# Weight blocks of 128x2048 instead of 128x1024 in a two-layer decoder, and what of it waits where

## The chip, the core and the metric

The kernel runs on one core of a Trainium2 chip. The metric is the device time of one execution in microseconds (us). Five engines work side by side and meet at semaphores: TensorE (PE in the profile, with PEld for its weight loads), VectorE (DVE), ScalarE (ACT), GpSimd (POOL) and SyncE (SP). DMA engines move data between DRAM and the on-chip memory; in this kernel SP issues the loads, POOL the loads that add to a tile, and ACT a few small ones.

## The reference

A decoder trunk of two layers on 256 tokens of width 2048. Layer 0 mixes tokens by gated linear attention, layer 1 by sliding-window attention; in both, four further heads attend to 256 memory tokens. A projection out, a residual and a squared-ReLU MLP (2048 to 8192 to 2048) follow. All in float32.

```python
for i in range(DEPTH):                                  # 2
    h = rmsnorm(x, attn_norm_g[i])
    mkv = mem_n @ w_mem_kv[i]                           # memory keys, values
    mk, mv = ...
    if i % 2 == 0:
        q, k, v, g_out, g_lr, xq = split(h @ w_in_gla)
        o_mix = rmsnorm(gla_mixer(q, k, v, g_lr, ...)) * silu(g_out)
    else:
        q, k, v, xq = split(h @ w_in_swa)
        o_mix = swa_sink_mixer(q, k, v, sinks)
    o_mem = memory_attention(xq, mk, mv)
    x = x + concatenate([o_mix, o_mem]) @ w_out[i]
    x = x + square(relu(rmsnorm(x) @ w_up[i])) @ w_down[i]
return rmsnorm(x, final_norm_g)
```

## The kernel before

**Every weight is used in two parts.** A weight block arrives in float32 (tile `wr`, by SP at L976), ACT copies it rounded to the format that TensorE reads (`wh`, the high half, L993), and DVE subtracts that copy from the block (`wl`, the low half, L994). Activations are stored split in the same way. A product is then three matmuls: high with high, high with low, low with high.

**Items.** The work is one list of items. An item is a block of 128 partitions by at most 1024 numbers, with what to do with it: load, perhaps a step before the split (`prep`), split, matmuls (`mm`), perhaps a step after the split (`then`). The main loop at the end of the kernel (L1013 to L1027) goes through the list with three leads: at item i it issues the load of item i+8 (LOAD_AHEAD), the `prep` of item i+5, the split of item i+3, then one step of each background task (softmax, gates, norms), then the matmuls of item i. There are 6 raw buffers (`wr`, WR) and 4 each of `wh` and `wl`. A scheduler then sets the order of the instructions on each engine, so this order is a plan and not the last word; the order shown below is that of the built program.

**The plans.** `fm_halves` (accumulators `p_acc`, `s_acc`; L198 and L199) makes two items for one block of 128 output columns: 8 pairs of a 512-wide and a 256-wide matmul each. `tm_halves` (`v_acc`, `o_acc`; L224 to L226) makes eight items for 512 output columns (388 for v), 12 matmuls each. `up` (L724 to L726) does the same for one of 16 up units of the MLP.

**Down projection.** It multiplies with sums of weight blocks: for each of seven groups e and each pair of column blocks, seven products take B11, T1, T2, B22, T3, T4 and B21 of the down weights (`FAST`, matmuls at L782 to L784). The T tiles are made by addition: `sum` is loaded with B11, then DVE adds B12 (`first_sum`, L828), then POOL adds B22 and later B21 by a DMA that accumulates (L825); `b12` is loaded with B12 and DVE adds the raw B22 block to it (`third_sum`, L831). Each accumulate must wait until the split of the sum before it is done. Group e is woven with the up units 2e+2 and 2e+3. The hidden units of an up unit pass through ACT and DVE (`q` at L755 to L758, `hid` at L762 and L763) before the down products read them. The last 1024 down rows go through `down_plain`.

**Start.** The first items of layer 0 are the x blocks and the v blocks, then memory blocks (`in_mem`, `in_mem_tok`, of which squares are taken, L141) placed among them and among the first gate, key and query blocks (`p0`, `p1`, ..., from `in_w_gla`). The memory keys and values of both layers are computed once in layer 0; those of layer 1 stay on the chip in `mk1` and `mv1`.

Of the kernel before, what the change touches and what calls it, by code (L numbers as in the profile page):

```python
# [16 lines left out]
P = 128  # L17
# [5 lines left out]
WR = 6  # L23
LOAD_AHEAD = 8
PREP_AHEAD = 5
SPLIT_AHEAD = 3
MEM_AT = (10, 15)
# [41 lines left out]
class Item:  # L69
# [5 lines left out]
    def __init__(self, src, width, split=None, mm=None, into=None, tile=None, prep=None, then=None):  # L75
        self.src, self.width, self.split, self.mm = src, width, split, mm
        self.into, self.tile, self.prep, self.then = into, tile, prep, then
# [3 lines left out]
def trunk_kernel(ctx: ExitStack, tc: tile.TileContext, a, out):  # L81
# [102 lines left out]
    def fm_halves(name, srcs, rhs, done, order=None):  # L184

        order = order or list(range(NK))
        st = {}

        def half(i):
            def mm(wh, wl):  # L190
                if i == 0:
                    st["acc"] = bank("main", name + "_acc")
                acc = st["acc"]
                r = rhs()
                for k in range(8):
                    kk = 8 * i + k
                    rk = r[order[kk]]
                    pe.matmul(acc, wh[:, k * P:(k + 1) * P], rk, start=kk == 0, stop=False, skip_group_check=True)  # L198
                    pe.matmul(acc[:, T:2 * T], wl[:, k * P:(k + 1) * P], rk[:, 0:T], start=False, stop=kk == NK - 1,  # L199
                              skip_group_check=True)  # L200
                if i == 1:
                    done(acc)
            return Item(srcs[i], 1024, mm=mm)

        return [half(0), half(1)]

    def tm_halves(name, srcs, n, lhs, done, order=None):
# [4 lines left out]
        def half(i):  # L212
            def mm(wh, wl):
                if i == 0:
                    st["acc"] = [bank("main", f"{name}_acc{t}") for t in range(2)]
                r = lhs()
                for t in range(2):
                    for k in range(2):
                        rk = r[order[2 * i + k]]
                        h, l = wh[:, k * n:(k + 1) * n], wl[:, k * n:(k + 1) * n]  # L220
                        first, last = 2 * i + k == 0, 2 * i + k == NK - 1
                        acc = st["acc"][t][:, 0:n]
                        hi, lo = rk[:, t * P:(t + 1) * P], rk[:, T + t * P:T + (t + 1) * P]
                        pe.matmul(acc, hi, h, start=first, stop=False)  # L224
                        pe.matmul(acc, hi, l, start=False, stop=False)  # L225
                        pe.matmul(acc, lo, h, start=False, stop=last)  # L226
                if i == 7:
                    done(st["acc"])
            return Item(srcs[i], 2 * n, mm=mm)

        return [half(i) for i in range(8)]

    def combine(acc, name):

        u = tp.tile([P, T], F32, tag="u", name=name + "_u")
        act.activation(u, acc[:, T:2 * T], AF.Copy)
        t = tp.tile([P, T], F32, tag="t", bufs=4, name=name + "_t")
# [18 lines left out]
    mkv = {1: [cp.tile([P, 4, T], F32, name="mk1"), cp.tile([P, 2, 512], F32, name="mv1")]}  # L256

    def act_item(src, first, n, key, gain, start=None):
# [9 lines left out]
        return Item(src, n * T, split=split)  # L268
# [21 lines left out]
    def x_task():  # L290

        for _ in range(4):
            yield
# [13 lines left out]
    def mem_halves(layer):  # L307
        hs = []

        def mv_done(accs):  # L310
            if layer == 0:
                S["mem_r"] = S["mem_st"].spread()
            for t in range(2):
                act.activation(mkv[layer][1][:, t, :], accs[t], AF.Copy, scale=S["mem_st"].tok[:, t:t + 1])

        hs += tm_halves(f"mv{layer}", [a["w_mv"][layer, i] for i in range(8)], 512, lambda: S["ms"], mv_done)
        for c in range(4):
            def mk_done(acc, c=c):
                t = combine(acc, f"mk{layer}{c}")
                dve.tensor_tensor(mkv[layer][0][:, c, :], t, S["mem_r"], ALU.mult)  # L320

            hs += fm_halves(f"mk{layer}{c}", [a["w_mk"][layer, c, i] for i in range(2)], lambda: S["ms"], mk_done)
# [40 lines left out]
    def gla_halves():  # L363
# [13 lines left out]
        vs = [tm_halves(f"v{g}", [a["w_v"][g, i] for i in range(8)], 388, lambda: S["xs"], v_done(g))  # L377
              for g in range(4)]
        for i in range(8):
            if i == 0:  # L380
                hs.append(act_item(a["x"][:, 0:2 * T], 0, 2, "xs", G_ATT))
            elif i == 1:
                hs.append(act_item(a["x"][:, 2 * T:4 * T], 2, 2, "xs", G_ATT))
            elif i % 2 == 0:
                hs.append(act_item(a["x"][:, 2 * i * T:(2 * i + 4) * T], 2 * i, 4, "xs", G_ATT))
            hs += [vs[0][i], vs[1][i]]
        rest = vs[2] + vs[3]
        extra = mem_items() + mem_stat_items()
        for i in range(16):
# [3 lines left out]
        def proj_done(job, idx):  # L393
            kind, h, j = job

            def f(acc):
# [15 lines left out]
                elif kind == "g":  # L412
                    sg = tp.tile([P, T], F32, tag="t", bufs=4, name=f"sg{idx}")
# [16 lines left out]
        for idx, job in enumerate(GLA_ORDER):  # L430
            if idx == 4:
                hs += mem_halves(0) + mem_halves(1)
            for h in fm_halves(f"p{idx}", [a["w_gla"][idx, i] for i in range(2)], lambda: S["xs"], proj_done(job, idx)):
                hs.append(h)
# [17 lines left out]
    def gla_task(h):  # L452
# [24 lines left out]
        ex = tp.tile([P, 2, P], F32, tag="t", bufs=4, name=f"ex{h}")  # L477
# [32 lines left out]
        for j in range(3):  # L510
# [6 lines left out]
            sq.append(tp.tile([P, T], F32, tag="sq", name=f"gsq{h}{j}", bufs=2))  # L517
# [8 lines left out]
        inv_sqrt(f"go{h}", b[:, 0:T], 1.0 / 384, r, *[tp.tile([P, T], F32, tag="t", bufs=4, name=f"go{h}_{z}") for z in "vw"])  # L526
# [6 lines left out]
    def start_swa():  # L533
# [14 lines left out]
        S["os"] = {}  # L548

# [76 lines left out]
    def swa_halves():  # L626
# [27 lines left out]
        jobs = [fm_halves(f"s{idx}", [a["w_swa"][idx, i] for i in range(2)], lambda: S["xs"], done(idx))  # L654
                for idx in range(len(SWA_COLS))]
        return late_start(jobs)


    def late_start(jobs):

        hs = [j[0] for j in jobs[0:3]] + [j[1] for j in jobs[0:3]]
        for j in jobs[3:]:
            hs += j
        return hs
# [22 lines left out]
    def out_halves(layer):  # L687
        hs = []
        for g in range(4):
            def done(accs, g=g):  # L690
# [3 lines left out]
            hs += tm_halves(f"o{layer}{g}", [a["w_out"][layer, g, i] for i in range(8)], 512, lambda: S["os"], done,  # L694
                            OUT_ROWS[layer])
        return hs

    def mlp_halves(layer):
# [9 lines left out]
        def up(n):  # L708

            st = {}  # L710

            def part(i):
                def mm(wh, wl):
                    if i == 0:
                        if n == 0:
                            open_phase()
                        st["acc"] = [bank("main" if n < 2 else "aux", f"u{layer}{n}_acc{t}") for t in range(2)]
                    for t in range(2):
                        for k in range(2):
                            rk = S["xs"][2 * i + k]  # L720
                            h, l = wh[:, k * 512:(k + 1) * 512], wl[:, k * 512:(k + 1) * 512]
                            hi, lo = rk[:, t * P:(t + 1) * P], rk[:, T + t * P:T + (t + 1) * P]
                            acc = st["acc"][t]
                            pe.matmul(acc, hi, h, start=2 * i + k == 0, stop=False)  # L724
                            pe.matmul(acc, hi, l, start=False, stop=False)  # L725
                            pe.matmul(acc, lo, h, start=False, stop=2 * i + k == NK - 1)  # L726
                    if i == 7:
                        p = S["phase"].pool.tile([P, 2, 512], F32, tag="relu", name=f"p{layer}{n}", bufs=1)
                        for t in range(2):
                            act.activation(p[:, t, :], st["acc"][t], AF.Relu, scale=S["st"].tok[:, t:t + 1])  # L730
                        making[n] = hid_task(n, p)
                        tasks.append(making[n])
                return Item(a["w_up"][layer, n, i], 1024, mm=mm)

            return [part(i) for i in range(8)]
# [42 lines left out]
        def products(acc, n, o, wh, wl, first, last):  # L778
            for c in range(2):
# [8 lines left out]
        def down_fast(e):  # L788


            def block(pair, u, name):
                return wd[layer, e, 2 * pair + int(name[2]) - 1, 2 * u + int(name[1]) - 1]

            def item(idx, u, pair):
                o, name, which, first, uses = FAST[idx]

                def mm(wh, wl):
                    if u == 0 and pair not in sums:
                        sums[pair] = {}
                    if u == 0 and which not in sums[pair]:  # L800
                        sums[pair][which] = bank("main", f"d{layer}{e}{pair}{which}")
                    acc = sums[pair][which]
                    products(acc, 2 * e + u, o, wh, wl, first and u == 0, u == 1)
                    if u == 1:
                        def take():
                            for t, col, sign in uses:
                                dst = x[t][2 * pair + col]
                                if sign > 0:
                                    dve.tensor_tensor(dst, acc, dst, ALU.add)
                                else:  # L810
                                    dve.tensor_tensor(dst, dst, acc, ALU.subtract)
                        later.append([1, take])

                def tile_of(kind):
                    return lambda *_: held[kind, pair, u]

                def new(kind):
                    def f():
                        held[kind, pair, u] = S["phase"].pool.tile([P, 1024], F32, tag=f"{kind}{pair}{u}",
                                                                   name=f"{kind}{layer}{e}{pair}{u}")  # L820
                        return held[kind, pair, u]
                    return f

                def plus(other):
                    return lambda raw: pool_e.dma_start(held["sum", pair, u], block(pair, u, other), accum_op=ALU.add)  # L825
# [275 lines left out]
```

## Time and profile before

| | us |
|---|---|
| three runs | 2108.70, 2109.93, 2111.22; median 2109.93 |
| the profiled execution | 2112.66, of which the span of the core is 2110.9 |
| ScalarE busy in the span | 1252.2 (59%) |
| VectorE busy | 1629.5 (77%) |
| TensorE busy | 2073.6 (98%) |
| GpSimd busy | 104.8 (5%) |
| mean granted TensorE clock | 0.998 of full speed |
| DRAM read | 453.24 MB, 216 GB/s over the span |

A matmul's end is modelled in the trace, so the time between the starts of two matmuls says more than the length of one. A line of waits names who waited, for whom, the microseconds in total, how often, and the longest.

### The profile page before, as it was taken

To read this page: it belongs to the slowest core of one execution; us is meant where nothing else is said; L and a number is where in the kernel's file an instruction comes from. 1 tells how busy PE (TensorE), PEld (TensorE's weight loads), DVE (VectorE), ACT (ScalarE), POOL (GpSimd) and SP (SyncE) were. 2 spreads that over 40 slices of the span, in tenths; PEclk is the share of its full clock that TensorE was granted. 3 is DMA by queue.
4 is the path that set the end of the run, shared out by engine and by line. 5 is a ranking of instruction groups with operands and counts; after the bars stand their busy time and mean duration, and the time that the engine had idled before them with its cause. 6 is when DMAs were issued, how large, how long until landed. Compare 5 with 4: busy or idle time off the path is not lost.

```text
span 2110.9 us, 27104 instructions
## 1 busy us (share of the span) xinstructions
PE 2073.6 (98%) x9902; PEld 1719.4 (81%) x9902; DVE 1629.5 (77%) x1993; ACT 1252.2 (59%) x1654; POOL 104.8 (5%) x138
## 2 busy tenths in 40 slices
PE   9999999999999999999999999999999999999998
PEld 9988888888787887877888887787787787877886
DVE  5655787556887988889887688557798887988975
ACT  6644666555666665666656466545566566665664
POOL 0000000000100101101000000000010100101100
PEclk9999999999999999999999999999999999999999
DMA  8856555566879879788776544575987879879773
GB/s 296 286 169 185 171 161 157 174 193 217 231 229 278 227 240 268 219 279 222 227 222 205 173 136 124 164 231 175 267 219 266 233 232 282 223 237 259 224 225 138
DMA packets 128150, 457.32 MB, mean 217 GB/s; under 512 B 14492, under 2 KB 14704, under 8 KB 128016
## 3 DMA queue, kind: packets, MB, share of 16 engines
q1 hardware_dynamic: 109872, 393.40, 56.8%
q0 software_dynamic: 16320, 58.81, 14.9%
q10 hardware_dynamic: 1824, 3.38, 0.5%
q8 instruction: 77, 1.26, 0.2%
q14 instruction: 57, 0.47, 0.1%
HBM read 453.24 MB, written 2.10 MB: 216 GB/s over the span
## 4 chain that ended last, share of the span: by engine, by line
PE 49%; issue 35%; DMA 9%; DVE 3%; ACT 2%; POOL 1%; SPq 0%; POOLq 0%; ACTq 0%; DVEq 0%
DMA sum<-in_w_down_dram 6%; PE p_acc L198 4%; PE s_acc L198 3%; PE u_acc L725 3%; PE u_acc L726 3%; PE u_acc L724 3%; DMA wr<-in_w_down_dram 3%; PE d L783 3%; PE d L782 3%; PE d L784 3%; DVE wl L994 2%; PE p_acc L199 2%; PE s_acc L199 2%; PE o_acc L224 1%; PE o_acc L225 1%
## 5 line engine op out<-in xcount | busy, mean ns | idle before, releaser
L994 DVE TENSOR_TENSOR wl<-wr,wh 128x1024 fp32r<-128x1024 f32 (+1 forms) x626 | 749.3, 1207 | 246.5 <-ACT wh L993 241.6
L993 ACT ACTIVATE wh<-wr 128x1024 fp32r<-128x1024 f32 (+1 forms) x626 | 651.6, 1047 | 435.9 <-PE o_acc L226 85.7
L725 PE MATMUL u_acc<-wl,mx 128*128 128x512 f32 x1024 | 400.3, 391 | 13.5 <-DVE wl L994 13.5
L724 PE MATMUL u_acc<-wh,mx 128*128 128x512 f32 x1024 | 399.8, 391 | 1.4 <-ACT wh L993 1.4
L726 PE MATMUL u_acc<-wh,mx 128*128 128x512 f32 x1024 | 398.7, 389 | 0.0
L993 ACT ACTIVATE wh<-sum 128x1024 fp32r<-128x1024 f32 x224 | 237.9, 1062 | 252.9 <-PE u_acc L726 160.6
L994 DVE TENSOR_TENSOR wl<-sum,wh 128x1024 fp32r<-128x1024 f32 x224 | 273.0, 1219 | 80.8 <-ACT wh L993 80.3
L783 PE MATMUL d<-wl,hid 128*128 128x512 f32 x784 | 309.7, 395 | 9.2 <-DVE wl L994 9.0
L782 PE MATMUL d<-wh,hid 128*128 128x512 f32 x784 | 308.5, 394 | 0.4 <-ACT hid L762 0.4
L784 PE MATMUL d<-wh,hid 128*128 128x512 f32 x784 | 304.5, 390 | 0.0
L725 PEld LDWEIGHTS u_acc<-wl,mx 128*128 128x128 f32 x1024 | 192.3, 188 | 58.8 <-DVE wl L994 19.5
L724 PEld LDWEIGHTS u_acc<-wh,mx 128*128 128x128 f32 x1024 | 192.1, 188 | 42.5 <-ACT wh L993 2.2
L726 PEld LDWEIGHTS u_acc<-wh,mx 128*128 128x128 f32 x1024 | 192.2, 188 | 39.9
L198 PE MATMUL p_acc<-ax,wh 128*128 128x512 f32 x512 | 183.9, 402 | 0.0
L783 PEld LDWEIGHTS d<-wl,hid 128*128 128x128 f32 x784 | 147.4, 188 | 44.5 <-DVE wl L994 15.6
L782 PEld LDWEIGHTS d<-wh,hid 128*128 128x128 f32 x784 | 147.2, 188 | 33.5 <-ACT hid L762 1.2
L784 PEld LDWEIGHTS d<-wh,hid 128*128 128x128 f32 x784 | 147.2, 188 | 32.3
L825 POOL DMA_DIRECT2D sum<-in_w_down_dram x112 | 95.6, 853 | 1496.3 <-DVE wl L994 1274.8
L199 PE MATMUL p_acc<-ax,wl 128*128 128x256 f32 x512 | 143.6, 281 | 0.0
L198 PEld LDWEIGHTS p_acc<-ax,wh 128*128 128x128 f32 x512 | 96.2, 188 | 23.7 <-ACT wh L993 1.0
L198 PE MATMUL s_acc<-ax,wh 128*128 128x512 f32 x304 | 111.3, 407 | 0.0
L831 DVE TENSOR_TENSOR b<-b,wr 128x1024 f32<-128x1024 f32 x56 | 68.3, 1220 | 45.9 <-DMA wr<-in_w_down_dram 45.9
(252 smaller groups left out, 2708.0 us busy)
## 6 DMA issues: line engine op xcount, KB each, us to landing
wr<-in_w_up_dram SPq DMA_DIRECT2D x256, 512.0 KB, 4.6
wr<-in_w_down_dram SPq DMA_DIRECT2D x144, 512.0 KB, 5.0
sum<-in_w_down_dram POOLq DMA_DIRECT2D x112, 512.0 KB, 9.7
wr<-in_w_gla_dram SPq DMA_DIRECT2D x64, 512.0 KB, 3.7
wr<-in_w_out_dram SPq DMA_DIRECT2D x64, 512.0 KB, 3.6
sum<-in_w_down_dram SPq DMA_DIRECT2D x56, 512.0 KB, 4.6
b<-in_w_down_dram SPq DMA_DIRECT2D x56, 512.0 KB, 5.1
wr<-in_w_swa_dram SPq DMA_DIRECT2D x38, 512.0 KB, 3.7
```

The source lines that it names most:

```text
L198: pe.matmul(acc, wh[:, k * P:(k + 1) * P], rk, start=kk == 0, stop=False, skip_group_check=True)
L199: pe.matmul(acc[:, T:2 * T], wl[:, k * P:(k + 1) * P], rk[:, 0:T], start=False, stop=kk == NK - 1, skip_group_check=True)
L724: pe.matmul(acc, hi, h, start=2 * i + k == 0, stop=False)
L725: pe.matmul(acc, hi, l, start=False, stop=False)
L726: pe.matmul(acc, lo, h, start=False, stop=2 * i + k == NK - 1)
L782: pe.matmul(acc, hi, h, start=first and c == 0, stop=False, skip_group_check=True)
L783: pe.matmul(acc, hi, l, start=False, stop=False, skip_group_check=True)
L784: pe.matmul(acc, lo, h, start=False, stop=last and c == 1, skip_group_check=True)
L825: return lambda raw: pool_e.dma_start(held["sum", pair, u], block(pair, u, other), accum_op=ALU.add)
L831: dve.tensor_tensor(held["b12", pair, u], held["b12", pair, u], raw, ALU.add)
L993: act.activation(hi[i][:, 0:w], r[:, 0:w], AF.Copy)
L994: dve.tensor_tensor(lo[i][:, 0:w], r[:, 0:w], hi[i][:, 0:w].bitcast(F32), ALU.subtract)
```

## The change

All blocks become up to 128x2048, so that there is half the number of loads, splits and weight sums (`WIDE`; `fm_items` and `tm_items` take the place of `fm_halves`, `tm_halves` and the loop in `up`). Only the first v items stay at 776. There are 3 raw buffers instead of 6 and 3 of each split half instead of 4, each of twice the size; the leads are 7, 3 and 2 items instead of 8, 5 and 3. The x blocks no longer use the raw buffers. The third sum moves ahead of the split's subtract (`use` instead of `then`), and a finished down product is taken into x one item earlier. Background tasks also step in the middle of an item.

The memory half of layer 1 is now computed first; its keys and values are written to DRAM (`keep_mkv`) and read back at the start of layer 1 (`fetch_mkv`). Temporaries `u`, `t`, `sq` come from the pool of their phase. The host lays the weights out in the new shapes. The numbers of matmuls stay.

```diff
-WR = 6
-LOAD_AHEAD = 8
-PREP_AHEAD = 5
-SPLIT_AHEAD = 3
-MEM_AT = (10, 15)
+WIDE = 2048
+WR = 3
+LOAD_AHEAD = 7
+PREP_AHEAD = 3
+SPLIT_AHEAD = 2
+MEM_AT = (4, 6, 7)
...
-    def tm_halves(name, srcs, n, lhs, done, order=None):
+    def tm_items(name, src, n, lhs, done, order=None, parts=(4, 4, 4, 4), tag="main"):
...
                 for t in range(2):
-                    for k in range(2):
-                        rk = r[order[2 * i + k]]
+                    if t == 1 and per == 4:
+                        step_tasks()
+                    for k in range(per):
+                        rk = r[order[c + k]]
...
+    def keep_mkv():
+
+        for i in range(2):
+            act.dma_start(kept[i], flat(1, i))
+
+    def fetch_mkv():
+        new_mkv(1)
+        for i in range(2):
+            act.dma_start(flat(1, i), kept[i])
...
-        vs = [tm_halves(f"v{g}", [a["w_v"][g, i] for i in range(8)], 388, lambda: S["xs"], v_done(g))
+        vs = [tm_items(f"v{g}", a["w_v"][g], 388, lambda: S["xs"], v_done(g), parts=(2, 2, 4, 4, 4) if g < 2 else (4,) * 4)
...
-                hs += mem_halves(0) + mem_halves(1)
+                hs += mem_halves(1) + mem_halves(0)
...
-                        later.append([1, take])
+                    later.append([0, take])
...
                 def third_sum(raw):
-                    dve.tensor_tensor(held["b12", pair, u], held["b12", pair, u], raw, ALU.add)
+                    s3 = held["b12", pair, e]
+                    dve.tensor_tensor(s3, s3, raw, ALU.add)
...
                 if name == "B22":
-                    return Item(block(pair, u, "B22"), 1024, mm=mm, then=third_sum)
+                    return Item(block(pair, "B22"), WIDE, mm=mm, use=third_sum)
...
-            return [item(idx, u, pair) for idx in range(7) for u in range(2) for pair in range(2)]
+            return [item(idx, pair) for idx in range(7) for pair in range(2)]
...
-            hs += woven(up(2 * e + 2) + up(2 * e + 3), down_fast(e), 4)
+            hs += woven(up(2 * e + 2) + up(2 * e + 3), down_fast(e), 2)
...
-        raw[i] = wp.tile([P, 1024], F32, tag="wr", name="wr", bufs=WR)
+        raw[i] = wp.tile([P, WIDE], F32, tag="wr", name="wr", bufs=WR)
...
-        hi[i] = wp.tile([P, 1024], F32R, tag="wh", name="wh", bufs=4)
-        lo[i] = wp.tile([P, 1024], F32R, tag="wl", name="wl", bufs=4)
-        act.activation(hi[i][:, 0:w], r[:, 0:w], AF.Copy)
-        dve.tensor_tensor(lo[i][:, 0:w], r[:, 0:w], hi[i][:, 0:w].bitcast(F32), ALU.subtract)
+        full = r[:, 0:w]
+        hi[i] = wp.tile([P, WIDE], F32R, tag="wh", name="wh", bufs=3)
+        lo[i] = wp.tile([P, WIDE], F32R, tag="wl", name="wl", bufs=3)
+        act.activation(hi[i][:, 0:w], full, AF.Copy)
+        if h.use:
+            h.use(full)
+        dve.tensor_tensor(lo[i][:, 0:w], full, hi[i][:, 0:w].bitcast(F32), ALU.subtract)
         if h.then:
-            h.then(r)
+            h.then()
```

Two places in the built program show what moves. The first is VectorE at the start of group e = 4 in layer 0's MLP, before. Names carry layer, group, pair and (before) half: `sum0400` is the sum tile of layer 0, group 4, pair 0, half 0; `q09` and `hid09` belong to up unit 9 of layer 0.

```order
L755 TENSOR_TENSOR q09_7495<-q09_7495 128x512
L994 TENSOR_TENSOR wl_7517<-wr_7431,wh_7516 128x1024
L994 TENSOR_TENSOR wl_7530<-sum0400_7443,wh_7529 128x1024
L757 SCALAR_TENSOR_TENSOR q09_7495<-q09_7495 128x256
L994 TENSOR_TENSOR wl_7548<-wr_7464,wh_7547 128x1024
L758 SCALAR_TENSOR_TENSOR q09_7495<-q09_7495 128x256
L994 TENSOR_TENSOR wl_7560<-sum0410_7476,wh_7559 128x1024
L809 TENSOR_TENSOR x00_256<-d0001_4978,x00_256 128x512
L809 TENSOR_TENSOR x02_300<-d0011_4991,x02_300 128x512
L763 TENSOR_TENSOR hid09_7533<-q09_7495,hid09_7533 128x7x256
```

Now, at the same place on VectorE:

```order
L774 TENSOR_TENSOR q09_6486<-q09_6486 128x512
L851 TENSOR_TENSOR sum040_6390<-sum040_6390,b12040_6460 128x2048
L776 SCALAR_TENSOR_TENSOR q09_6486<-q09_6486 128x256
L1022 TENSOR_TENSOR wl_6571<-sum041_6442,wh_6570 128x2048
L777 SCALAR_TENSOR_TENSOR q09_6486<-q09_6486 128x256
L851 TENSOR_TENSOR sum041_6442<-sum041_6442,b12041_6511 128x2048
L782 TENSOR_TENSOR hid09_6537<-q09_6486,hid09_6537 128x7x256
L1022 TENSOR_TENSOR wl_6587<-sum040_6390,wh_6586 128x2048
L831 TENSOR_TENSOR x00_204<-d0000_4364,x00_204 128x512
L1022 TENSOR_TENSOR wl_6620<-wr_6479,wh_6619 128x2048
```

Between the steps that make the hidden units there now stand whole 2048-wide pieces, and both first sums have moved between them. On ScalarE before, at that place:

```order
L993 ACTIVATE wh_7529<-sum0400_7443 128x1024
L993 ACTIVATE wh_7547<-wr_7464 128x1024
L993 ACTIVATE wh_7559<-sum0410_7476 128x1024
L762 ACTIVATE hid09_7533<-q09_7495 128x7x256
L993 ACTIVATE wh_7580<-sum0401_7488 128x1024
```

and now:

```order
L1019 ACTIVATE wh_6513<-sum040_6390 128x2048
L1019 ACTIVATE wh_6532<-wr_6408 128x2048
L1019 ACTIVATE wh_6570<-sum041_6442 128x2048
L781 ACTIVATE hid09_6537<-q09_6486 128x7x256
L1019 ACTIVATE wh_6586<-sum040_6390 128x2048
```

The same pieces stand ahead of `hid09`, each twice as wide. The second place is SP's queue at the entry to the key, query and gate blocks (`in_w_gla`) of layer 0, before:

```order
L976 DMA wr_741<-in_w_gla_dram 128x1024
L976 DMA wr_759<-in_mem_dram 128x1024
L976 DMA wr_765<-in_w_gla_dram 128x1024
L976 DMA wr_783<-in_mem_dram 128x1024
L976 DMA wr_801<-in_w_gla_dram 128x1024
L976 DMA wr_823<-in_mem_tok_dram 128x1024
L976 DMA wr_841<-in_w_gla_dram 128x1024
L976 DMA wr_865<-in_mem_tok_dram 128x1024
L976 DMA wr_871<-in_w_gla_dram 128x1024
```

and now:

```order
L1001 DMA wr_643<-in_w_gla_dram 128x2048
L1001 DMA wr_675<-in_mem_dram 128x1024
L1001 DMA wr_681<-in_mem_tok_dram 128x1024
L1001 DMA wr_715<-in_w_gla_dram 128x2048
L1001 DMA wr_745<-in_mem_tok_dram 128x1024
L1001 DMA wr_755<-in_mem_tok_dram 128x1024
L1001 DMA wr_787<-in_w_gla_dram 128x2048
L1001 DMA wr_797<-in_mem_tok_dram 128x1024
L1001 DMA wr_852<-in_w_gla_dram 128x2048
```

Each memory block takes one of three wide raw buffers though it fills half of it, and two stand between two gate blocks where one stood between two halves.

More of the change, by code (lines that the diff above doesn't have):

```diff
@@ L182, in trunk_kernel, with fm_items, part @@
     tasks = []
-    def fm_halves(name, srcs, rhs, done, order=None):
-        order = order or list(range(NK))
+    def fm_items(name, src, rhs, done, parts=1):
         st = {}
-        def half(i):
+        n = NK // parts
+        def part(i):
             def mm(wh, wl):
@@ L290, in x_task @@
     def x_task():
-        for _ in range(4):
+        for _ in range(2):
             yield
@@ L799, in mm @@
                         sums[pair] = {}
-                    if u == 0 and which not in sums[pair]:
+                    if which not in sums[pair]:
                         sums[pair][which] = bank("main", f"d{layer}{e}{pair}{which}")
                     acc = sums[pair][which]
[L803 to L811, printed above, removed]
-                        later.append([1, take])
+                    for u in range(2):
+                        cols = slice(1024 * u, 1024 * u + 1024)
+                        products(acc, 2 * e + u, o, wh[:, cols], wl[:, cols], first and u == 0, u == 1)
```

232 lines of the change are left out of this document (120 added, 112 removed).

## The prediction

> **What bounds the kernel now.** I read the page's busy times and chain first, then TensorE's waits, then the windows of the phases. The columns of a window are the stretch, its length, busy time of PE, PEld, DVE, ACT and POOL, the granted clock, the DMA share and GB/s.
>
> ```profile
> PE 2073.6 (98%) x9902; PEld 1719.4 (81%) x9902; DVE 1629.5 (77%) x1993; ACT 1252.2 (59%) x1654; POOL 104.8 (5%) x138
> PE 49%; issue 35%; DMA 9%; DVE 3%; ACT 2%; POOL 1%; SPq 0%; POOLq 0%; ACTq 0%; DVEq 0%
> PE u_acc L725 <- DVE wl L994: 13.5, 12, 1.2
> PE d L783 <- DVE wl L994: 9.0, 13, 1.6
> PE u_acc L724 <- ACT wh L993: 1.4, 2, 0.7
> 450.00:500.00 50.00, 50.00 (x224) 41.06 (x223) 27.05 (x33) 22.63 (x31) 0.00 (x0) 1.00 0.80 269
> 650.00:700.00 50.00, 47.98 (x213) 38.94 (x212) 42.30 (x43) 31.66 (x32) 0.00 (x0) 1.00 0.77 258
> 1250.00:1300.00 50.00, 50.00 (x327) 39.29 (x326) 42.62 (x109) 32.11 (x90) 0.00 (x0) 1.00 0.44 127
> ```
>
> PE is busy for 2073.6 of 2110.9 us at the full clock, so 37.3 us at most can be won without taking matmuls away, and the change takes none away. In the out-projection (450 to 500) and the window attention (1250 to 1300) PE is busy without a gap; in the MLP (650 to 700) it idles 2.0 in 50. The three waits say where: 13.5 + 9.0 + 1.4 = 23.9 us, 27 events, nearly all for the low half of a split weight, all in the two MLPs. Over 14 woven groups that is 1.7 each. A modelled matmul end hides some 0.16 more of each event (0.39 shown against a step of 0.23, below), so 1.9 to 2.1 per group and 27 to 29 in all could be removed.
>
> **Prices.** PE steps, splits and sums:
>
> ```profile
> 621.28 0.39 PE L782 MATMUL d<-wh,hid 128*128 128x512 f32 x1
> 624.02 0.39 PE L724 MATMUL u_acc<-wh,mx 128*128 128x512 f32 x1
> 626.74 0.39 PE L782 MATMUL d<-wh,hid 128*128 128x512 f32 x1
> L994 DVE TENSOR_TENSOR wl<-wr,wh 128x1024 fp32r<-128x1024 f32 x594 | 718.5, 1220 | 226.8 <-ACT wh L993 222.0 <-PE p_acc L199 0.6
> L763 DVE TENSOR_TENSOR hid<-q,hid 128x1792 fp32r<-128x1792 f32 x28 | 56.5, 2018 | 8.3 <-ACT hid L762 8.3
> 643.95 3.49 DVE L994 TENSOR_TENSOR wl<-wr,wh 128x1024 fp32r<-128x1024 f32 x3
> L993 ACT ACTIVATE wh<-wr 128x1024 fp32r<-128x1024 f32 x594 | 624.7, 1058 | 423.4 <-PE o_acc L226 85.7 <-PE u_acc L726 73.6 <-PE p_acc L198 60.5
> L762 ACT ACTIVATE hid<-q 128x1792 fp32r<-128x1792 f32 x28 | 47.7, 1704 | 42.9 <-DVE q L758 42.9
> L757 DVE SCALAR_TENSOR_TENSOR q<-q 128x256 f32<-128x256 f32 x28 | 11.7, 418 | 0.1
> L831 DVE TENSOR_TENSOR b<-b,wr 128x1024 f32<-128x1024 f32 x56 | 68.3, 1220 | 45.9 <-DMA wr<-in_w_down_dram 45.9
> ```
>
> Twelve matmuls take 2.74 (down) and 2.72 (up), so a wide up item (24) is 5.45 us of PE, a wide down item (12) 2.75. Carrying the line from 1024 to 1792 on to 2048 gives a wide high half 1.92 on ACT and a wide low half 2.29 on DVE. Three narrow subtracts in a row take 3.49, so one step is (3.49 - 1.22)/2 = 1.135 and a wide one about 2.2: joining two saves DVE 0.07 us, not 0.15. The latency from a raw block to its low half grows from 1.06 + 1.22 = 2.28 to 1.92 + 2.29 = 4.2.
>
> Transfers (KB each, us from issue to landing), the wait of SP's queue, and three sums in a row on ACT:
>
> ```profile
> wr<-in_w_up_dram SPq DMA_DIRECT2D x256, 512.0 KB, 4.6
> wr<-in_w_down_dram SPq DMA_DIRECT2D x144, 512.0 KB, 5.0
> wr<-in_w_out_dram SPq DMA_DIRECT2D x64, 512.0 KB, 3.6
> sum<-in_w_down_dram POOLq DMA_DIRECT2D x112, 512.0 KB, 9.7
> q1 hardware_dynamic: 109872, 393.40, 56.8%
> SPq L976 <- DVE wl L994: 1342.5, 512, 10.3
> 631.19 1.07 ACT L993 ACTIVATE wh<-sum 128x1024 fp32r<-128x1024 f32 x1 [1.80 <-DMA sum<-in_w_down_dram]
> 635.03 1.06 ACT L993 ACTIVATE wh<-sum 128x1024 fp32r<-128x1024 f32 x1 [1.56 <-DMA sum<-in_w_down_dram]
> 638.84 1.06 ACT L993 ACTIVATE wh<-sum 128x1024 fp32r<-128x1024 f32 x1 [2.75 <-DMA sum<-in_w_down_dram]
> ```
>
> A packet of q1 (3.6 KB) occupies an engine for 0.568 x 16 x 2110.9/109872 = 0.175 us; 8 per engine make 1.4 of the 3.6. A load of 1 MB is not in the trace. Alone it takes an estimated 3.6 + 1.4 = 5.0; doubled outright, 10. I take 7.8, the 5.0 plus twice the 1.4 us by which MLP loads are slower than out-projection ones. Accumulates in series land 3.8 apart (631.19, 635.03, 638.84), so 7.6 for a wide one.
>
> **The change, part by part.**
>
> *Fewer, wider splits.* Per group 44 pairs become 22, 4 first sums become 2, 4 third sums 2. DVE saves about 2 of the 84 us that a group lasts (8 x 5.45 + 14 x 2.75 = 82, and 2 for transposes), ACT more. None of that is on PE's path: the window at 450 has DVE at 54% and PE without a gap. It pays only where a late split is late because DVE is behind.
>
> *Half as many buffers of twice the size.* A split may run while PE does two items (5.5 to 8.2 us) and needs 4.2; before, three narrow ones (4.1 to 6.8) against 2.3. SP's queue waited 1342.5 us for raw buffers and stays the waiting one; the bytes ahead are equal, in 3 pieces.
>
> *A steady MLP group*, walked from the order. u0 to u7 are its wide up items, d0 to d13 its products, two column pairs for each of A11·B11, T1, T2, B22, T3, T4, B21; time 0 is PE's start on u0. (1) The hidden activations of the last up unit: their ACT step needs two 0.42 us steps of DVE that now stand behind whole wide pieces, and DVE's d1 piece cannot start before u0 has freed a buffer at 5.7; they come at 12.5, wanted at 12.05: 0.45. (2) d2 takes the buffer that u1 frees at 13.45: high half 15.4, low half 17.7, wanted 17.1: 0.6. (3) T2 of pair 1 needs the second wide accumulate: issued at 22.7 behind a first that lands at 26, it lands 33.5, low half 37.8, wanted 36.8: 1.0, which moves one for one with the accumulate. (4) Third sum of pair 1: it waits for a load issued at 40.9 that lands 48.7 and, now ahead of the subtracts on DVE, delays the next up split by 0.6 (0 with a 5.0 us load, 2.7 with 10). Each event also makes the next matmul 0.1 longer: 0.4. Sum 3.05 for 2.0 before: **+1.1 in each of 12 groups, +13**. Bounds: -27 if all vanish, +45 with (3) and (4) at their worst. I take the walk's value, since it lies nearest to what the same waits cost now.
>
> *First group of each layer*, which has no runway: +1 each, +2.
>
> *The start and the entry to the gate projections:*
>
> ```profile
> wr<-in_w_v_dram SPq DMA_DIRECT2D x32, 388.0 KB, 4.6
> 9.31 0.97 DVE L994 TENSOR_TENSOR wl<-wr,wh 128x776 fp32r<-128x776 f32 x1 [0.95 <-ACT wh L993]
> 11.90 0.33 PE L224 MATMUL v_acc<-wh,ax 128*128 128x388 f32 x1
> 15.97 0.34 PE L224 MATMUL v_acc<-wh,ax 128*128 128x388 f32 x1
> 77.05 0.63 ACT L141 ACTIVATE mem_sq<-wr 128x512 f32<-128x512 f32 x1 [1.65 <-DMA wr<-in_mem_tok_dram]
> 80.00:90.00 10.00, 10.00 (x62) 8.83 (x61) 6.35 (x10) 9.57 (x21) 0.00 (x0) 1.00 1.01 365
> 85.92 0.39 PE L198 MATMUL p_acc<-ax,wh 128*128 128x512 f32 x1
> 91.46 0.39 PE L198 MATMUL p_acc<-ax,wh 128*128 128x512 f32 x1
> ```
>
> 23 steps of v take 4.07, so 0.177 each. The first wide v block needs the raw buffer that the subtract at 9.31 frees at 10.3; it lands 5.6 to 9.2 later (16 to 19.5), its low half 3.2 after that (19 to 22.7), and PE, with 36 narrow steps done, wants it at 17.5: +3 (1.5 to 5). At the entry, 16 pairs of p take 5.54. Counted from PE's start on the last v block but two, p0's low half is done at 11.7; only that frees the buffer of p1, which lands at 16.7 to 19.4 (DMA engines full there: 1.01), low half 21 to 23.6, wanted at 18.3: 3.5. p2's buffer is held by a memory block until its squares are done at 21: about 2.5 more. p3's high half stands behind gate work on ACT: 1. **+7 (3 to 9)**. Before, six buffers let the memory blocks lie beside the loads, and PE had no gap in 80 to 90.
>
> *At nothing.* Memory keys and values to DRAM and back: 2 MB the fetch in the phase whose DMA share is 0.44, on ACT's queue, wanted some 14 us after the fetch is issued; uncovered they cost two landings, 8 us. Temporaries moved to the phase pool: same tiles, same counts; final gains in one load; tasks stepped inside an item: same instructions, PE does not wait for them at 1250. Uncovered, each costs one wait of 1 us or less.
>
> **Sum.** 3 + 7 + 13 + 2 = +25 on a profiled execution of 2112.66 (span 2110.9), which is 2.7 above the median of 2109.93: 2137.7, or **2135** on the median's scale.
>
> **Rivals.** "Same" means within 0.2%, 4 us, what a measurement of this kernel tells from no change (its runs spread over 2.5).
> - *Faster: the MLP waits vanish.* In 650 to 700 DVE is busy 85%, so the low halves may be late because DVE is behind; 2 us less work a group and a runway of two wide items then absorb it. -28 in the MLPs, +3 to +10 before them: 2085 to 2094. It decides where the four waits of the walk come to under 1.2 a group. Against it: (2) is set by a buffer, not by DVE's load. 0.30.
> - *Half of that:* the gain pays the entry, 2106 to 2114. 0.10.
> - *MLP unchanged, entry only:* 2118 to 2122. 0.10.
> - *A wide load costs little more than a narrow one*: 1.4 more, 6.2 in the MLP. Then the third sum's 0.6 goes, entry shrinks to 4: 3 + 4 + 12 x 0.45 + 2 = +15, 2125. 0.12. The Trainium skill (DMA: Bandwidth & Descriptors, the table in "Anatomy of one DMA") prices a transfer at about 2.0 us fixed plus bytes at 436 GB/s, from which I estimate 3.2 us for 512 KB and 4.4 for 1 MB. The trace's 3.6 in the out-projection is close to it, the 5.0 in the MLP and the 9.7 of the accumulates are not.
> - *Accumulates land a further 3.8 late* because two wide ones collide with wide loads: (3) becomes 4.8 a group, 14 x 3.8 = +53, minus what (4) then hides, 2165 to 2185. 0.10.
> - *Forecast,* 2127 to 2150: 0.28.
>
> The change not doing what it says: the DVE time it saves is 14 x 2 = 28 us of 1630 that PE hardly waits for; that is the forecast's and the third rival's case.
>
> **How the numbers follow.** Faster 0.30, same 0.10, slower 0.10 + 0.12 + 0.28 + 0.10 = 0.60. The range runs from 2088, inside the first rival, to 2170, inside the late accumulates; it leaves out about 0.15. The likeliest case's own range is 2127 to 2150.
>
> **What would show it.** In the changed profile: matmul waits of some 40 us in the MLP by events of up to 1 us, the largest behind `wl` of the sum tiles; matmuls of `p_acc` waiting about 7 us near 90 to 110, where none do now; one wait of about 3 near 17; wide `wl` at 2.2 to 2.3 and `wh` at 1.9; 1 MB loads at 7 to 8. The out-projection and the window attention keep PE without a gap. I am wrong if the MLP window shows PE at 49.5 of 50 or more, or if wide loads land in under 6.

## The result and the profile after

The changed kernel takes 2178.49 us in the median of four runs (2174.58 to 2180.07), the kernel before 2109.31 in four on the same chip. The ratio is 1.0325, with a 95% interval of 1.0307 to 1.0343: 69 us slower, where 25 were forecast, and 8 us above the range. The profiled execution of after took 2174.58 us (span 2172.9), that of before 2112.66 (2110.9); the spans differ by 62.

The page of after, busy times and packets, and the two kinds of transfer that matter. The last lines are the issues: KB each and median us to landing.

```profile
PE 2098.8 (97%) x9902; PEld 1722.1 (79%) x9902; DVE 1578.0 (73%) x1489; ACT 1173.7 (54%) x1206; POOL 59.6 (3%) x82
q1 hardware_dynamic: 57888, 393.37, 50.4%
wr<-in_w_up_dram SPq DMA_DIRECT2D x128, 1024.0 KB, 6.3
wr<-in_w_down_dram SPq DMA_DIRECT2D x70, 1024.0 KB, 5.9
sum<-in_w_down_dram POOLq DMA_DIRECT2D x56, 1024.0 KB, 8.8
wr<-in_w_out_dram SPq DMA_DIRECT2D x32, 1024.0 KB, 4.9
```

All that the change set out to make less has become less: DVE has 51 us less work, ACT 79, the packets are half, and a load of twice the size lands 0.9 to 1.7 us later (1.3 in the out-projection), not twice as late. PE idles 74.1 us instead of 37.3 and is busy 25.2 longer for the same matmuls. Its waits (us in total, times, longest):

```profile
PE d L803 <- DVE wl L1022: 38.0, 40, 2.2
PE u_acc L231 <- DVE wl L1022: 9.2, 12, 1.1
PE d L802 <- ACT wh L1019: 4.9, 7, 1.1
PE d L802 <- ACT hid L781: 2.5, 4, 1.1
PE p_acc L204 <- DVE wl L1022: 2.5, 2, 1.5
PE v_acc L230 <- ACT wh L1019: 1.9, 2, 1.6
PE v_acc L231 <- DVE wl L1022: 1.4, 1, 1.4
```

The wait of the up products got shorter (13.5 to 9.2); that of the down products on a low half grew from 9.0 to 38.0, and waits on a high half joined it. One group shows how. It is group e = 5 of layer 0, whose first matmul (u0) is at 976.94. In the timeline, first what POOL issues (the two accumulates of B22; those of B21 follow at 1011.90 and 1017.58), then SP's queue, ACT, DVE and PE (start, length, instruction, and in brackets the idle time before it and what ended it):

```profile
994.65 0.86 POOL L847 DMA_DIRECT2D sum<-in_w_down_dram  x1 [66.35 <-DVE wl L1022]
999.79 0.85 POOL L847 DMA_DIRECT2D sum<-in_w_down_dram  x1 [4.29 <-DVE wl L1022]
...
997.18 0.33 SPq L1001 DMA_DIRECT2D wr<-in_w_down_dram  x1
1002.18 0.33 SPq L1001 DMA_DIRECT2D wr<-in_w_up_dram  x1
...
1003.37 1.92 ACT L1019 ACTIVATE wh<-sum 128x2048 fp32r<-128x2048 f32 x1 [4.21 <-DMA sum<-in_w_down_dram]
1013.05 1.91 ACT L1019 ACTIVATE wh<-sum 128x2048 fp32r<-128x2048 f32 x1 [7.76 <-DMA sum<-in_w_down_dram]
...
1007.11 2.29 DVE L855 TENSOR_TENSOR b<-b,wr 128x2048 f32<-128x2048 f32 x1 [4.36 <-DMA wr<-in_w_down_dram]
1009.32 2.28 DVE L1022 TENSOR_TENSOR wl<-sum,wh 128x2048 fp32r<-128x2048 f32 x1
1014.99 2.29 DVE L1022 TENSOR_TENSOR wl<-sum,wh 128x2048 fp32r<-128x2048 f32 x1 [3.39 <-ACT wh L1019]
...
1011.66 0.50 PE L803 MATMUL d<-wl,hid 128*128 128x512 f32 x1 [0.57 <-DVE wl L1022]
1015.01 0.51 PE L802 MATMUL d<-wh,hid 128*128 128x512 f32 x1 [0.55 <-ACT wh L1019]
1017.34 0.50 PE L803 MATMUL d<-wl,hid 128*128 128x512 f32 x1 [1.82 <-DVE wl L1022]
```

The first accumulate lands about 1003.3, 8.6 us after its issue. The second, issued at 999.79, has landed at 1013.05, 13.3 us later; only then can ACT begin its wide high half, DVE the low half, and PE goes on at 1017.34. In between B22's load for the third sum, issued at 997.18, lands at 1007.1, 9.9 us later, and T2's other low half, whose high half was ready at 1005.3, stands behind that third sum on DVE. The DMA engines are nearly full through it (the number before the last), in after (first line, from the first accumulate's issue to the second's landing) and in the same stretch of a group before (second):

```profile
994.65:1013.05 18.40, 17.83 (x78) 14.37 (x78) 12.59 (x8) 5.70 (x5) 2.56 (x3) 1.00 0.89 229
```

```profile
962.50:981.20 18.70, 18.70 (x84) 15.43 (x83) 18.31 (x18) 9.65 (x10) 5.96 (x7) 1.00 0.97 236
```

The rate is the same, 229 and 236 GB/s, and both kernels need some 18 us until the sums of a group have taken in B22. Before, four pieces of 512 KB landed one after another in that time, and each was split and used as it came; PE was busy for all of the 18.70. Here are the first issue of that group and ACT's four high halves of the sums that have taken in B22:

```profile
962.55 0.85 POOL L825 DMA_DIRECT2D sum<-in_w_down_dram  x1 [63.46 <-DVE wl L994]
...
970.35 1.07 ACT L993 ACTIVATE wh<-sum 128x1024 fp32r<-128x1024 f32 x1 [1.66 <-PE u_acc L726]
974.39 1.07 ACT L993 ACTIVATE wh<-sum 128x1024 fp32r<-128x1024 f32 x1 [1.65 <-PE u_acc L726]
977.14 1.07 ACT L993 ACTIVATE wh<-sum 128x1024 fp32r<-128x1024 f32 x1 [0.31 <-PE d L784]
980.80 1.06 ACT L993 ACTIVATE wh<-sum 128x1024 fp32r<-128x1024 f32 x1 [2.60 <-DMA sum<-in_w_down_dram]
```

Now there are two pieces, and nothing of the second can be used until all of it is there.

A second effect stands in no wait. After some gaps of 1.1 to 2.2 us, most with a shorter one just before, the granted clock falls to half for some 3 us (windows in after around the gap that ends at 927.20; the third number from the end is the clock):

```profile
925.00:927.50 2.50, 0.68 (x2) 0.36 (x3) 2.50 (x2) 2.50 (x3) 0.06 (x1) 0.96 0.97 200
927.50:930.00 2.50, 2.50 (x7) 1.92 (x7) 2.45 (x2) 2.06 (x2) 0.79 (x1) 0.50 1.13 206
930.00:932.50 2.50, 2.50 (x15) 2.11 (x14) 2.50 (x3) 0.89 (x1) 0.00 (x0) 0.85 0.96 193
```

Six matmuls start in the middle 2.5 us instead of eleven (the x7 counts one that had begun before). Six such stretches in this execution lost 8.0 us (steps of 0.42 against 0.23, summed), counted as busy time. PE's extra 25.2 us are mostly these 8.0 and, for each of 43 more waits, some 0.27 that a wait adds to the busy time as the prediction had it (0.16 hidden by a modelled end and 0.11 in a longer next step), another 11.6.

### The profile page after: what moved, and what is told of

It reads as the page before. It is cut to its first block, busy times and chain, and to the rows that moved or that the text cites. A ratio compares the mean times of both kernels' runs of the same rounds, so it can differ in the third digit from the quotient of the medians.

```text
span 2172.9 us, 24587 instructions
## 1 busy us (share of the span) xinstructions
PE 2098.8 (97%) x9902; PEld 1722.1 (79%) x9902; DVE 1578.0 (73%) x1489; ACT 1173.7 (54%) x1206; POOL 59.6 (3%) x82
## 4 chain that ended last, share of the span: by engine, by line
PE 53%; DMA 15%; issue 13%; DVE 13%; ACT 5%; POOL 0%; ACTq 0%; DVEq 0%; SPq 0%; POOLq 0%
DVE wl L1022 9%; DMA wr<-in_w_down_dram 7%; DMA sum<-in_w_down_dram 6%; PE u_acc L231 6%; PE u_acc L232 5%; PE u_acc L230 5%; ACT wh L1019 4%; PE d L802 4%; PE d L803 4%; PE d L804 3%; PE p_acc L203 3%; PE s_acc L203 3%; PE p_acc L204 2%; PE s_acc L204 2%; PE o_acc L230 1%
## 5 line engine op out<-in xcount | busy, mean ns | idle before, releaser
L1022 DVE TENSOR_TENSOR wl<-wr,wh 128x2048 fp32r<-128x2048 f32 (+3 forms) x318 | 706.2, 2228 | 303.5 <-ACT wh L1019 296.6
L1019 ACT ACTIVATE wh<-wr 128x2048 fp32r<-128x2048 f32 (+3 forms) x318 | 592.3, 1867 | 410.5 <-DMA wr<-in_w_down_dram 85.7
L1019 ACT ACTIVATE wh<-sum 128x2048 fp32r<-128x2048 f32 x112 | 215.2, 1921 | 302.0 <-DMA sum<-in_w_down_dram 146.5
L803 PE MATMUL d<-wl,hid 128*128 128x512 f32 x784 | 315.5, 403 | 38.7 <-DVE wl L1022 38.0
L802 PE MATMUL d<-wh,hid 128*128 128x512 f32 x784 | 314.0, 400 | 7.7 <-ACT wh L1019 4.9
L1022 DVE TENSOR_TENSOR wl<-sum,wh 128x2048 fp32r<-128x2048 f32 x112 | 256.4, 2289 | 87.9 <-ACT wh L1019 87.0
L804 PE MATMUL d<-wh,hid 128*128 128x512 f32 x784 | 306.4, 394 | 0.0
L855 DVE TENSOR_TENSOR b<-b,wr 128x2048 f32<-128x2048 f32 x28 | 64.2, 2292 | 101.5 <-DMA wr<-in_w_down_dram 101.5
L230 PE MATMUL o_acc<-wh,os 128*128 128x512 f32 x256 | 102.3, 400 | 0.0
```

The costliest lines, as they stand in the source:

```text
L230: pe.matmul(acc, hi, h, start=c + k == 0, stop=False)
L802: pe.matmul(acc, hi, h, start=first and c == 0, stop=False, skip_group_check=True)
L803: pe.matmul(acc, hi, l, start=False, stop=False, skip_group_check=True)
L804: pe.matmul(acc, lo, h, start=False, stop=last and c == 1, skip_group_check=True)
L855: dve.tensor_tensor(s3, s3, raw, ALU.add)
L1019: act.activation(hi[i][:, 0:w], full, AF.Copy)
```

## Experiments

Theories. **A**: the accumulates; a wide sum is handed from split to accumulate to next split only as a whole, while its transfers share nearly full DMA engines. **B**: the third sum stands on DVE ahead of T2's low half and waits for its load. **C**: a wide split takes 4.2 us, more than its buffers allow. Times are medians; the ratio with its interval is to the kernel before on the same chip (2109 to 2110 us).

**No accumulate traffic.** T2 and T4 are not the right sums here.

```diff
-                    return lambda: pool_e.dma_start(held["sum", pair, e], block(pair, other), accum_op=ALU.add)
+                    return lambda: pool_e.dma_start(held["sum", pair, e][:, 0:64], block(pair, other)[:, 0:64], accum_op=ALU.add)
```

> The wide kernel with the accumulates cut to 64 of 2048 columns, so that T2 and T4 are not the right sums: the same instructions in the same order, but 57 MB of accumulate traffic is left out. Theory A: the waits on T2 go and B22's load lands in 5 to 6 us, so the waits of the third sum on DVE (101 us) fall below 30; 2125 to 2140. Theory B: the same, since the load that it waits for is quicker. Theory C: the waits on T2 were only a part; more than half of the 70 us stays, 2155 or more.

2116.44 us, 1.0029 [1.0020, 1.0039]: 62 of the 69 us are gone, with the orders on PE, DVE and ACT as in after. Its waits on PE and, last, that of the third sum on DVE (101.5 us in after):

```profile
PE d L803 <- DVE wl L1022: 5.7, 12, 0.5
PE d L802 <- ACT wh L1019: 3.4, 4, 1.1
PE p_acc L204 <- DVE wl L1022: 2.9, 2, 1.5
...
DVE b L855 <- DMA wr<-in_w_down_dram: 4.0, 4, 2.0
```

Theory C is left with 12 waits of up to 0.5 us, one in each steady group (d2 of the prediction). A and B both survive, since the load that B speaks of is quick here too.

**Third sum behind T2.** A one-column step makes it wait for T2's low halves.

```diff
-                    s3 = held["b12", pair, e]
+                    s3, after = held["b12", pair, e], recent[pair - 2]
+                    dve.scalar_tensor_tensor(s3[:, 0:1], after[:, 0:1].bitcast(F32), 0.0, s3[:, 0:1], ALU.mult, ALU.add)
```

> The wide kernel with the third sum forced behind both low halves of T2 on DVE (a one-column DVE step that reads the low half times zero makes it wait). Theory A: only the wait on T2 of pair 0 goes (some 8 to 12 us of the group waits), T2 of pair 1 still waits for its accumulate; 2163 to 2175. Theory B: the waits on both T2 products go; 2140 to 2150. Theory C: no change, or slower because the raw buffer of B22 is held longer.

2177.44 us, 1.0316 [1.0300, 1.0332], no change, and 2 us above what A had allowed. The third sum's wait fell from 101.5 to 20.4 us. T2 of pair 0 no longer waits in the steady groups, but T2 of pair 1 waits about as much more:

```profile
PE d L803 <- DVE wl L1024: 28.4, 25, 1.8
PE d L802 <- ACT wh L1021: 12.2, 16, 1.5
```

This fits that the landing of the second accumulate sets the time, and that the wait on DVE before it only took some of that time early. B is out as the cause. PE idles 4 us less than in after (69.9) but is busy 5.5 longer (2104.3), because the waits now lie in one place and more of the time passes at half clock (mean granted clock 0.989 here, 0.994 in after). That is more than the 2 us by which A's bound was missed.

**B22 ahead of T2.**

```diff
-        (S2, "T2", 0, False, [(0, 1, -1)]),
         (S4, "B22", 1, False, [(0, 1, -1)]),
+        (S2, "T2", 0, False, [(0, 1, -1)]),
```

> The wide kernel with the product B22 moved ahead of T2 in each group, so that each accumulate has two more products (5.5 us) and an up item (5.45 us) to land in, and B22's load runs before the accumulates instead of beside them. Theory A (the accumulates are late: the second one lands 13.1 us after its issue because two wide accumulates, B22's load and an up load share the DMA engines): the waits on T2 (27 us in all, and most of the half-clock stretches behind them, 10 us) go; 2178 falls to 2135 to 2150. Theory B (the third sum stands on DVE ahead of T2's low half and waits for B22's load): the third sum still stands ahead of other low halves and waits for its load; 2160 or more. Theory C (a wide split takes 4.2 us where its buffer allows less): nothing changes, 2170 or more.

2163.28 us, 1.0253 [1.0233, 1.0273]: 15 us gained, where A expected 28 or more; by itself the time is what B had allowed. The waits on T2 went, but B22's product of pair 0 now waits 0.9 to 2.5 us a group in their place, and up items wait on a high half (10.4 us in all) that did not before. Earlier loads alone move the collision.

**Splits in halves.**

```diff
-        act.activation(hi[i][:, 0:w], full, AF.Copy)
+        cuts = [(0, w)] if w <= 1024 else [(0, w // 2), (w // 2, w)]
+        for c0, c1 in cuts:
+            act.activation(hi[i][:, c0:c1], full[:, c0:c1], AF.Copy)
         if h.use:
             h.use(full)
-        dve.tensor_tensor(lo[i][:, 0:w], full, hi[i][:, 0:w].bitcast(F32), ALU.subtract)
+        for c0, c1 in cuts:
+            dve.tensor_tensor(lo[i][:, c0:c1], full[:, c0:c1], hi[i][:, c0:c1].bitcast(F32), ALU.subtract)
```

> The wide kernel with each wide split done as two 1024-wide pieces on ACT and on DVE; loads, buffers and accumulates stay wide. The first low half comes after 2.3 us instead of 4.2, the second after 3.5 to 4.5. Theory C: nearly all waits go; 2120 to 2135. Theories A and B: each of some 40 waits shrinks by 1 to 1.9 us, those of T2 (up to 2.8) stay in part; 2140 to 2160.

2138.90 us, 1.0137 [1.0115, 1.0160], 1 us below what A and B allowed and 4 above what C did, so it decides little by itself: each wait shrinks, and the half-clock stretches behind the MLP's waits are gone (clock 0.999). T2 still waits (PE waits 22.6 us on low halves of down products), and the third sum waits 102.5 us as before.

**Accumulates in halves**, with whole and with halved splits:

```diff
-                    return lambda: pool_e.dma_start(held["sum", pair, e], block(pair, other), accum_op=ALU.add)
+                    def f():
+                        for c in (0, 1024):
+                            pool_e.dma_start(held["sum", pair, e][:, c:c + 1024], block(pair, other)[:, c:c + 1024],
+                                             accum_op=ALU.add)
+                    return f
```

> The wide kernel with each 1 MB accumulate issued as two of 512 KB, one behind the other; splits stay wide. If the cause is the bytes that share the DMA engines, or that a sum must have landed whole before its wide split starts (A1), nothing is gained: 2172 to 2185. If a single 1 MB accumulate is slow by itself, as one transfer (A2), the halves land sooner and the waits on T2 shrink by half: 2150 to 2160.

> Wide splits done in two pieces and accumulates issued in two pieces, so that a half's accumulate starts when that half is split, and the next split starts when that half has landed; loads, raw buffers and third sums stay wide. A1 (what was lost is the pipelining between split, accumulate and next split in 1024-wide steps): the waits on T2, 18 us left with half splits alone, go; 2112 to 2125, and what stays is the third sum's wait. If the bytes on the DMA engines are the cause, no change against half splits alone: 2134 to 2142.

Accumulates alone: 2207.94 us, 1.0468 [1.0453, 1.0484], 30 us slower than after, outside both expectations, part of it at half clock (mean 0.984). A group's B22 sums land 19 to 20 us after the first issue instead of 17.2 to 18.3, and nothing uses the halves that land early. With both in halves: 2117.30 us, 1.0038 [1.0026, 1.0050], though the sums land just as late (18.6 to 19.8 in the steady groups). The waits of the kernel with both:

```profile
PE u_acc L231 <- DVE wl L1029: 13.0, 13, 1.2
PE d L803 <- DVE wl L1029: 6.6, 19, 0.8
```

The same DMAs cost 30 us where a whole wide split must wait for both halves and give 22 (2138.9 to 2117.3) where each half goes on by itself. That is the hand-over of theory A, and what is left is the third sum's wait, 13.0 us on up items, as in the kernel before (13.5). The buffers and leads of the change stay in this kernel, so they are not the main cost.

**Loads in halves.**

```diff
-        nc.sync.dma_start(raw[i][:, 0:h.width], h.src)
+        halves(raw[i][:, 0:h.width], h.src, h.width)
...
+    def halves(dst, src, w):
+        for c in range(0, w, 1024):
+            d = min(c + 1024, w)
+            nc.sync.dma_start(dst[:, c:d], src[:, c:d])
```

> The wide kernel with every load of over 1024 columns issued by SP as two DMAs of up to 512 KB into the same wide buffer; accumulates, splits and buffers stay wide. If the size of a single load is what makes the accumulates and the third sum's load late, 2130 to 2150. If it is the same bytes and the wide hand-over from split to accumulate to split, no change: 2170 to 2190.

2210.62 us, 1.0481 [1.0464, 1.0499], 32 us slower than after and above both expectations. The third sum's wait, and T2's:

```profile
DVE b L855 <- DMA wr<-in_w_down_dram: 150.3, 28, 9.6
...
PE d L803 <- DVE wl L1027: 56.5, 31, 5.9
```

In group 5 the halves of B22's load land 10.5 and 15.4 us after the first accumulate's issue, where the whole one landed at 12.4. So the large loads were not what hurt; cut in two, the piece that matters ends later. Why the second half falls back was not tried.

**Memory part alone**, on the kernel before: `keep_mkv`, `fetch_mkv`, the order of the memory halves and the phase's temporaries, as in the change.

> The kernel before (all blocks 1024 wide, 6 raw buffers) with only that part of the change that frees memory: layer 1's memory keys and values go to DRAM and come back, its memory half is computed first, temporaries live in their phase's pool. The prediction took it at nothing: 2105 to 2114. If the fetch or the phase's temporaries put a wait on TensorE's path, 2115 to 2120.

2106.52 us, 0.9986 [0.9977, 0.9995]: at nothing, as forecast, or 2.5 us better. It was run in the narrow kernel alone, and there it is no part of the 69.

**B22 ahead of T2 where hand-over is fine**: in the kernel with both in halves, and in the kernel before (the same two-line edit).

> As before, and the product B22 ahead of T2, so that B22's load runs before the accumulates. If the third sum's wait for a load that collides with the accumulates is what stays (the waits of up items of 1.3 us in each group), it goes too: 2100 to 2112. Otherwise as without the swap.

> The kernel before (all blocks 1024 wide), with the product B22 ahead of T2 and nothing else. Its waits are 13.5 us on up items, one of 1.33 in nearly every group behind the third sum on DVE, and 9 us on down items. If they come from B22's load colliding with the accumulates, they go: 2090 to 2098. If the swap only moves the collision, 2105 to 2113.

2100.89 us, 0.9957 [0.9941, 0.9974], and 2082.49 us, 0.9870 [0.9855, 0.9884]. The second is the fastest kernel of the study, 27 us under the kernel before and 8 below what was expected. PE's longest waits in it, the third sum's group (no idle time ahead of it), and its MLP windows:

```profile
PE v_acc L224 <- ACT wh L993: 1.9, 2, 1.3
PE u_acc L724 <- ACT wh L993: 1.4, 2, 0.7
PE warm L117 <- DVE ones L108: 1.1, 1, 1.1
PE d L782 <- ACT hid L762: 0.4, 2, 0.2
```

```profile
L831 DVE TENSOR_TENSOR b<-b,wr 128x1024 f32<-128x1024 f32 x56 | 68.3, 1220 | 0.0
```

```profile
650.00:700.00 50.00, 50.00 (x225) 41.28 (x224) 42.52 (x43) 32.11 (x33) 0.85 (x1) 1.00 0.77 244
700.00:750.00 50.00, 50.00 (x226) 41.33 (x225) 45.89 (x46) 31.28 (x31) 6.82 (x8) 1.00 0.99 281
```

All of the 22.5 us for which PE waited on low halves in the kernel before are gone, though DVE is as busy as it was and an accumulate still takes 8.2 us in the median (9.7). This fits that its waits came from B22's load and the accumulates being under way together, and from the third sum standing on DVE until that load came. The swap also gives each accumulate more products to land behind, and these two effects were not told apart. Of the 18 us between this kernel and the wide one with all cures, 17 arise in the two MLPs (by the starts of the same matmuls); what they are was not followed.

## Why the prediction was right and wrong

- *Direction* was right, and so was the kind of cause: DVE's saving lay off the path, and the splits' waits in the MLP grew. Their size was not.
- *Prices* held: 1.92 and 2.29 for a wide split (measured 1.92 and 2.29), 5.0 for a lone 1 MB load (4.9). MLP loads land in 5.9 to 6.3, not 7.8, in the median; the one beside the accumulates in group 5 takes 9.9, the 10 of the upper bound. Wide loads that land in under 6 were named as a sign of being wrong; the down loads did (5.9), but the result was slower than forecast and not faster, so the sign was a poor one.
- *The steady group* is the step that failed, +13 forecast. By the starts of the same matmuls, after is 5.5 us late where the first MLP begins, 36.1 where it ends, 36.3 where the second begins and 62.6 where that ends: the MLPs cost 57 us where the forecast had 15. Term by term in group 5, as time lost between two starts: (1) 0.45 forecast, nothing measured. (2) 0.6, measured 0.68. (4) 0.6, measured 0.63. (3) 1.0, measured 2.10 + 0.73, and T2 of pair 0 with 0.74 has no term at all. Together that is 4.9 us for the 2.65 of the four terms; the longer next steps come on top in both. The walk had the issues right (17.7 and 22.7 us after u0; measured 17.7 and 22.9) and the first landing (26; 26.4), but the second accumulate lands at 36.1, not 33.5. Term (3) moves one for one with it: 1.0 and 2.6 more are 3.6, and the three waits on T2 are 3.57. So the mis-sized term is that landing. It was priced at two 3.8 us steps behind the first, which leaves 15.8 us from the first issue to the second landing. The same 2 MB had taken 18.2 in the group before that is shown above (962.55 to 980.80), and they take 17.2 to 18.3 in after, 17.7 in the mean, with a load of B22 and one of an up item beside them. From this I estimate 1.9 us a group, 23 of the 42 that the forecast lacks in the MLPs; half clock is another 7, and the rest was not taken apart. On DVE the third sum of pair 0 stands in front of T2's low half (1007.11 and 1009.32 above); the walk only asked what it does to pair 1.
- *Half clock* was in no term, 8 us here (one of the six stretches at the start, five in the MLPs), since the kernel before has no MLP wait after which it falls.
- *First groups*, +2 forecast: in 500 to 550 PE is busy 46.35 of 50 at a mean clock of 0.95 (before, 47.98 at 1.00), which is more than that:

```profile
500.00:550.00 50.00, 46.35 (x196) 36.49 (x195) 33.48 (x23) 24.68 (x19) 1.01 (x2) 0.95 0.41 117
```

- *Start and entry*, +3 and +7: by the starts of the same matmuls the start lost 3.3, as forecast, and the entry 3.1, half of what was forecast, with two waits at p1 and p2 (2.5 us) where they were placed. The kernel without accumulates, which keeps these and the first groups, is 6.5 us slower than before in all.
- *Rivals.* The late accumulates had 0.10 and 2165 to 2185, which holds the result; the range stopped inside it, at 2170. Its mechanism is the measured one, but not its size (3.8 us a group, 1.4 to 2.5 against the walk here): half clock filled up the time, so the hit is in part luck. The Trainium skill's price (DMA: Bandwidth & Descriptors, "Anatomy of one DMA", given there for transfers that GpSimd issues), an estimate of 4.4 us for 1 MB, is near the 4.9 of a lone load, which SP issued; beside the accumulates 9.9 and 13.3 were measured, so it holds here only for a transfer that has the engines to itself. The rival built on cheap wide loads was right on the loads and missed the result by 53 us.

## What to carry to other kernels

Where a block goes through several steps with transfers between (split, accumulate, split again), its width is the unit of the hand-over: twice as wide halves the instructions and doubles what must be complete before anything goes on, at an unchanged transfer rate. Look for the chain whose transfers run when the DMA engines are already nearly full, and price its last landing with everything that is in flight then, not by the median of its kind. Before making work cheaper on an engine off the path, try moving the colliding load: two lines in the order of the products gave 27 us here.

## What the hardware showed that was not expected

- Half the clock after short gaps: 1.82 us of idle (after 0.82 and 0.14 in the 6 us before) or 2.22 us alone were enough, while others of 1.8 to 2.0 us passed without it. Each stretch lost 1.2 to 1.4 us over some 3 us. The profile's record of the granted clock holds a likely reason: each stretch lasts 3.41 us, and their starts lie whole multiples of 3.413 us apart. In the 3.41 us ahead of each of the five in the MLPs PE stood idle for 2.0 to 2.4 us in all, counted as time between two starts beyond the usual 0.23, and in no other piece of that grid after the start for more than 1.98. So it seems that idle time is summed piece by piece, and a gap across a border counts in two; in the MLPs of the other wide kernels the border lies between 1.9 and 2.1, and no run tested it. The Trainium skill (TensorE: Matmul & The Clock Gate, "HAM oscillation") warns of idle gaps above about 3.4 us; here gaps of two thirds of that sufficed.
- With accumulates under way the DMA engines were at 0.89 to 0.97 of their time and moved 229 to 236 GB/s; in a stretch of plain loads before, at 80 to 90 us, they moved 365 at 1.01.
- The same transfer in two DMAs was not neutral: accumulates in halves landed some 2 us later as a set, and the second half of B22's load 3 us later than the whole.
